# HGRN value tiles as one token-major group, and modulation products over 512 inputs per instruction, in a two-layer trunk kernel

## The chip, the cores and the metric

One core of a Trainium2 chip runs the whole kernel. The metric is the device time in microseconds (us) of one execution, the median of three runs. TensorE is called PE in the profile (its weight loads PEld), VectorE DVE, ScalarE ACT, GpSimd POOL, and SyncE, which here only issues transfers, SP.

## The reference

Two layers run over 640 tokens (128 of context, 512 latent) with a model width of 2048. Each layer modulates its input, makes one wide projection, feeds three branches from it, gates the branches and projects back:

```python
m = jax.nn.silu(cond) @ ada_w_l + ada_b_l            # "modulation": shift, scale, gate, 2048 each,
shift, scale, gate = jnp.split(m, 3, axis=-1)         # for two conditions (context, latent)
h = x * (1 + scale) + shift
z = h @ w_in_l                                        # 640 x 6656
aq, ak, av, ag, hq, hi, hff, hfb, hgate, ca, cb, cgate = jnp.split(z, SPLIT_POINTS, axis=-1)
v = hi.reshape(B, L, HG_HEADS, HG_DV)                 # HGRN values, 4 heads of 128
S_new = exp(g_last)[..., None] * S + einsum('bhsd,bhse->bhde', kc * exp(g_last - G), vc)
u = ca * jax.nn.sigmoid(cb)                           # conv branch: 31 taps, LayerNorm, silu
mix = concat([att * silu(ag), hg_out * silu(hgate), cv_out * silu(cgate)])
out = mix @ w_out_l
x_new = layer_norm(ALPHA * x + gate * out, ln_w_l, ln_b_l)
```

`hi` (512 columns) is the value of the HGRN branch; the scan needs it with tokens on the partitions.

## The kernel before

**Projection.** All products are in fp32, each operand split into a high and a low part, so that one product is three matmuls: input high by weight high (HH, wh), input low by weight high (HL, wh), input high by weight low. The 52 column tiles of 128 (`NTILES`, L32 ff.) are computed one after the other by `mm` (L1162 ff.): the weight tile is stationary, the 640 tokens stream as a matmul of 256 columns (L1173) and one of 384 (L1175), 16 k-blocks by 3, 48 pairs a tile. The result is feature-major (features on partitions) in one of two double banks `zt`. The tiles come in the order `hff, hfb, hi, hq` of the four heads, `hgate`, attention, `cb`/`ca`, `ag`, and at the end of the layer the four `cgate`.

**Weights.** Each tile's weights come in four chunks of 256 KB into the `RAW` slots (SP queue), and `ahead` splits the chunks of the next tile into the `WH` slots while this tile runs (ACT twice at L290/L291, and an accumulating DMA issued by POOL at L292).

**Everything else** is written as Python generators. `pump(3, rate)`, called after every half chunk, eight times a tile, lets up to three generators emit their next step, and also, `rate` times on the average, one step of the modulation job. The order in which the generators emit is the order in which each engine executes; nothing is reordered later. If a tile needs a free `zt` bank, `pump_until` (ahead of each tile) lets generators emit steps until one is free; where none can move, it takes a step of the modulation job instead.

**Slots.** Scratch comes from the pool `S` of 9 slots. `conv_ln` (L1030 ff.) holds the four conv sums and two more, `r` and `r2`, and at `summed()` takes two more at once, `S.getn`, before it can go on: a split (L287), PE sums over channels (L426, L427), 12 DVE products (L1068), squares on ACT (L1072), sums (L1046 to L1048), the same split and PE sums again, Ln (L1080), Exp (L1082), products (L1085), silu (L1091). `e_gate` takes one `S` slot before it evacuates its tile's `zt` bank (L1096), and holds it until the branch it gates is ready: for the `cgate` tiles this is the end of `conv_ln`.

**HGRN values.** `e_hi` evacuates a `hi` tile, and `to_tokens` turns it by five PE transposes (L474, L478), each copied out by ACT.

**Modulation.** The first layer's shift and scale are computed by PE at the start (`ada_pe`, L317 ff.; 16 steps of 256 features, on each of which `after0` builds part of the first layer's input). The other four parts are jobs of `ada_dve` (L336 ff.): two in layer 0 for its own gate and for layer 1's scale and shift among them, one in layer 1. A job has 64 raw weight blocks of 128x512 (256 KB, `adawD`), each multiplied with a row of the silu of a condition that is the same on all partitions (`crow`, 256 KB for 256 inputs of both conditions, L352), 4 products of 128x256 a block with a running sum (L362). A row occupies one `S` slot for 8 blocks, and the next one is loaded ahead, when half of the blocks are done.

**Start and boundary.** In the start three tiles run under `ada_pe` as its steps finish (`start_mm`). Between the layers, the last columns of the output projection (L1482) of each of the five token tiles are followed by `ln_next` (LayerNorm, modulation and transposes at L1384 of the next input), and next to it the first two tiles of the next layer run.

## Time and profile before

| what | value |
|---|---|
| median of three runs | 2241.13 us (2240.1 to 2241.21) |
| profiled execution, its own time | 2247.12 us |
| its span (first to last instruction) | 2245.3 us |
| PE busy / DVE / ACT / POOL | 97% / 65% / 51% / 27% |
| mean granted TensorE clock (share of 2.4 GHz) | 0.994 |

The profile is of one execution, so sums are made against its 2247.12 us and then set against the median. Busy shares come per engine; the page also gives them in forty slices of the span. The durations of matmuls overlap, since they are pipelined: what one costs is the distance from its start to the next one's start, which the timeline shows.

### The profile page before, as it was taken

The numbers are of one execution on the slowest core, as the hardware profiler recorded it, in microseconds if no ns is written. First come the engines' busy times: TensorE is split into PE (matmuls) and PEld (weight loads), VectorE is DVE, ScalarE is ACT, GpSimd is POOL, SyncE is SP. The second block draws the span as 40 slices with busy tenths as digits, with TensorE's granted clock in tenths as the row PEclk, the third lists the DMA queues.
The fourth block names the chain that finished last, engine by engine and source line by source line (L and its number), as shares of the span: only waits on it lengthen the run. The fifth ranks groups of instructions, "written<-read, shape, count | busy, mean of one in ns | idle before, by whom it ended". The sixth has DMA issues, their size and how long they took to land.

```text
span 2245.3 us, 42128 instructions
## 1 busy us (share of the span) xinstructions
PE 2177.4 (97%) x15854; PEld 2076.1 (92%) x15854; DVE 1457.9 (65%) x3799; ACT 1144.7 (51%) x2051; POOL 601.9 (27%) x690
## 2 busy tenths in 40 slices
PE   5899999999999999999989999999999999999997
PEld 2699999999999999988989999999999999998887
DVE  2478899557669999766673666543654779225457
ACT  1267877546565435511155787774555543462112
POOL 0033344332222343300032344433222123331003
PEclk9999999999999999999999999999999999999999
DMA  9978787897766888964426777778776576676333
GB/s 358 392 206 199 185 209 182 201 219 173 176 159 155 206 193 212 259 233 128 128 108 158 156 172 162 162 173 189 160 163 137 110 173 147 150 164 212 99 99 123
DMA packets 210557, 403.61 MB, mean 180 GB/s; under 512 B 24656, under 2 KB 30512, under 8 KB 209712
## 3 DMA queue, kind: packets, MB, share of 16 engines
q1 hardware_dynamic: 138992, 271.85, 38.4%
q0 software_dynamic: 61440, 116.96, 30.2%
q10 hardware_dynamic: 9920, 12.10, 1.7%
q8 instruction: 124, 2.03, 0.4%
q14 instruction: 81, 0.66, 0.1%
HBM read 383.46 MB, written 12.11 MB: 176 GB/s over the span
## 4 chain that ended last, share of the span: by engine, by line
PE 75%; DVE 9%; DMA 6%; issue 5%; ACT 3%; POOL 1%; ACTq 1%; SPq 0%; POOLq 0%; DVEq 0%
PE z L1175 29%; PE z L1173 19%; PE z L1431 9%; PE m L1431 8%; DVE junk L362 4%; DMA x<-adaw 2%; PE m L948 2%; PE m L1482 2%; PE m L862 1%; DMA s<-xT 1%; PE m L916 1%; DMA s<-s 1%; DMA wh<-win 1%; PE m L664 1%; ACT s L1391 1%
## 5 line engine op out<-in xcount | busy, mean ns | idle before, releaser
L1175 PE MATMUL z<-HH,wh 128*128 128x384 f32 x3296 | 1046.6, 339 | 0.0
L1173 PE MATMUL z<-HH,wh 128*128 128x256 f32 x3296 | 926.6, 283 | 1.9 <-DMA wh<-win 1.0
L292 POOL DMA_DIRECT2D wh<-win x388 | 345.2, 936 | 1095.3 <-ACT wh L291 1024.0
L1173 PEld LDWEIGHTS z<-HH,wh 128*128 128x128 f32 x3296 | 619.5, 189 | 5.8 <-DVE wh L287 1.6
L1175 PEld LDWEIGHTS z<-HH,wh 128*128 128x128 f32 x3296 | 620.6, 188 | 1.5
L1175 PE MATMUL z<-HL,wh 128*128 128x384 f32 x1648 | 558.2, 339 | 0.0
L362 DVE SCALAR_TENSOR_TENSOR junk<-raw,s 128x256 bf16<-128x256 f32 x1024 | 502.5, 491 | 53.2 <-DMA raw<-adawD 25.0
L1173 PE MATMUL z<-HL,wh 128*128 128x256 f32 x1648 | 461.6, 280 | 0.0
L1173 PEld LDWEIGHTS z<-HL,wh 128*128 128x128 f32 x1648 | 310.9, 189 | 0.0
L1175 PEld LDWEIGHTS z<-HL,wh 128*128 128x128 f32 x1648 | 310.4, 188 | 0.0
L291 ACT ACTIVATE wh<-wh 128x512 fp32r<-128x512 f32 x400 | 253.0, 633 | 78.5 <-PE z L1175 67.4
L290 ACT CAST wh<-raw 128x512 fp32r<-128x512 f32 x400 | 244.0, 610 | 72.0 <-issue 36.1
L286 ACT CAST wh<-raw 128x512 fp32r<-128x512 f32 x136 | 83.0, 621 | 305.0 <-PE m L1431 153.8
L1027 DVE SCALAR_TENSOR_TENSOR s<-s,sm,s 128x655 f32<-128x655 f32 x240 | 229.6, 957 | 6.3
L1431 PE MATMUL z<-wh,HH 128*128 128x512 f32 (+1 forms) x640 | 182.1, 368 | 0.0
L1431 PE MATMUL m<-wh,HH 128*128 128x512 f32 (+1 forms) x640 | 173.8, 357 | 0.0
L287 DVE TENSOR_TENSOR wh<-raw,wh 128x512 fp32r<-128x512 f32 x138 | 92.6, 687 | 119.5 <-ACT wh L286 119.5
L1431 PEld LDWEIGHTS z<-wh,HH 128*128 128x128 f32 x640 | 116.1, 189 | 20.1
L1431 PEld LDWEIGHTS m<-wh,HH 128*128 128x128 f32 x640 | 114.2, 189 | 17.6
L1431 PE MATMUL z<-wh,HL 128*128 128x512 f32 (+1 forms) x320 | 117.8, 368 | 0.0
L1431 PE MATMUL m<-wh,HL 128*128 128x512 f32 (+1 forms) x320 | 114.4, 358 | 0.0
L1096 ACT ACTIVATE s<-z 128x640 f32<-128x640 f32 x32 | 22.5, 703 | 152.5 <-PE z L1175 143.7
(561 smaller groups left out, 2718.6 us busy)
## 6 DMA issues: line engine op xcount, KB each, us to landing
raw<-win SPq DMA_DIRECT2D x416, 256.0 KB, 4.2
wh<-win POOLq DMA_DIRECT2D x388, 256.0 KB, 5.6
raw<-adawD SPq DMA_DIRECT2D x256, 256.0 KB, 4.2
x<-adaw SPq DMA_DIRECT2D x64, 512.0 KB, 8.3
raw<-wout SPq DMA_DIRECT2D x128, 256.0 KB, 2.7
s<-crow SPq DMA_DIRECT2D x32, 256.0 KB, 5.9
s<-xT ACTq DMA_DIRECT2D x16, 320.0 KB, 7.5
s<-s ACTq DMA_DIRECT2D x80, 64.0 KB, 3.9
```

The lines of the kernel that those rows point to most:

```text
L286: act.copy(hi, src)
L287: (lo_eng or dve).tensor_tensor(lo, src, hi.bitcast(F32), op=ALU.subtract)
L290: act.copy(hi, r)
L291: act.activation(lo, hi.bitcast(F32), AF.Copy, scale=-1.0)
L292: pool.dma_start(out=lo, in_=w.bitcast(F32R), accum_op=ALU.add)
L362: dve.scalar_tensor_tensor(junk, r[:, 256 * n:256 * n + 256], 1.0, rows[0][:, 256 * c:256 * c + 256], op0=ALU.mult, op1=ALU.mult, accum_ou ...
L948: pe.matmul(o, lhsT=v_, rhs=p_, start=(y == 0 and n_ == 0), stop=(y == len(bl) - 1 and n_ == 2))
L1027: dve.scalar_tensor_tensor(acc, u[:, t:t + AW], sm[:, cw + t:cw + t + 1], acc, op0=ALU.mult, op1=ALU.add)
L1173: pe.matmul(za, lhsT=w_, rhs=h_[:, 0:2, k, :], start=st_, stop=sp_)
L1175: pe.matmul(zb, lhsT=w_, rhs=h_[:, 2:5, k, :], start=st_, stop=sp_)
L1431: pe.matmul(bs[tt][:, 0:w], lhsT=h_[:, tt, k, :], rhs=w_[:, o:o + w], start=(k == 0 and n_ == 0), stop=(k == KT - 1 and n_ == 2))
L1482: pe.matmul(b[:, 0:w], lhsT=h_[:, tt, k, :], rhs=w_[:, o:o + w], start=(k == 0 and n_ == 0), stop=(k == KT - 1 and n_ == 2))
```

## The change

Two things change together.

The four `hi` tiles of a layer are no longer single tiles. They are computed as one group ahead of the 48 other tiles, with the input as the stationary operand and 512 weight columns streaming (`mm_hi`: 16 k-blocks, 5 token tiles, 3 matmuls of 512 columns, 240 a layer), so that the result has tokens on the partitions at once. `evac_hi` copies the five banks to where the output of the HGRN branch will be, and the separate value tile, `e_hi` and the transposes go. The order of tiles has the `hgate` tiles between the others, and the first tile goes to two single banks. At the start the group runs under `ada_pe` in place of the three tiles, with 16 weight chunks by the sixth of eight steps (12 before); at the boundary the group takes the place of the first two tiles, and its weight chunks 0 to 7 are split by POOL alone and by ACT with an accumulating DMA in turn.

In `ada_dve` a block is now multiplied by two products of 128x512 (one for each condition) in place of four of 128x256. A row is 512 inputs of one condition; two `S` slots hold both conditions' rows for 16 blocks, and the next two are taken and loaded where the former two are given back. Line numbers of the changed kernel are a few off: L362 is L371 there, L352 L365, L426/L427 L435/L436, L1068 L1062, L1173/L1175 L1167/L1169.

```diff
     def ada_dve(l, part):
         pi = ADAD.index((l, part))
-        rows, fly = deque(), deque()
-        tiles = [(kb, q) for kb in range(8) for q in range(8)]
-        nrow = nxt = 0
+        fly = deque()
+        tiles = [(kb, q) for kb in range(4) for q in range(KT)]
+        nxt = 0
         for kb, q in tiles:
...
-            if nrow <= kb or (nrow <= min(kb + 1, 7) and q == 4):
-                t = yield from S.get()
-                sync.dma_start(out=t[:, 0:512], in_=crow[nrow].rearrange("c k -> (c k)").partition_broadcast(P))
-                rows.append(t)
-                nrow += 1
-            yield
+            if q == 0:
+                rows = yield from S.getn(F32, F32)
+                for c in range(2):
+                    sync.dma_start(out=rows[c][:, 0:512], in_=crow[kb, c].partition_broadcast(P))
+                yield
             r = fly.popleft()
-            for n in range(2):
-                if n:
-                    yield
-                for c in range(2):
-                    o = 2 * (2 * q + n) + c
-                    dve.scalar_tensor_tensor(junk, r[:, 256 * n:256 * n + 256], 1.0, rows[0][:, 256 * c:256 * c + 256],
-                                             op0=ALU.mult, op1=ALU.mult, accum_out=aacc[:, kb, o:o + 1])
+            for c in range(2):
+                yield
+                o = 2 * q + c
+                dve.scalar_tensor_tensor(junk, r, 1.0, rows[c][:, 0:512], op0=ALU.mult, op1=ALU.mult,
+                                         accum_out=aacc[:, kb, o:o + 1])
             RAW.put(r)
-            if q == 7:
-                S.put(rows.popleft())
+            if q == KT - 1:
+                S.put(*rows)
...
+    def evac_hi(l, G):
+        h = outs[l][2]["h"].rearrange("p (j t) -> p j t", j=4)
+        for c in (1, 4, 0, 3, 2):
+            o, i = h[:, :, 128 * c:128 * c + 128], G[c].rearrange("p (j t) -> p j t", j=4)
+            if c > 2:
+                dve.tensor_copy(o, i)
+            else:
+                act.copy(o, i)
...
+    def mm_hi(l, G, k, tts):
+        hi, lo = wsp[l, k]
+        for tt in tts:
+            for n_, (h_, w_) in enumerate(((HH, hi), (HH, lo), (HL, hi))):
+                pe.matmul(G[tt], lhsT=h_[:, tt, k, :], rhs=w_, start=(k == 0 and n_ == 0),
+                          stop=(k == KT - 1 and n_ == 2))
...
     def start_mm(n):
-        for i in range(NS):
-            mm(0, i, zs[i], (2 * n, 2 * n + 1), (0, 1))
-            if n % 2:
-                WH.put(*wsp.pop((0, i, n // 2)))
+        for k in (2 * n, 2 * n + 1):
+            mm_hi(0, G, k, range(TT))
+            WH.put(*wsp.pop((0, k)))
...
-            rate = RATE[l][0 if i < 20 else 1 if i < 32 else 2 if i < 45 else 3]
+            rate = RATE[l][0 if i < 16 else 1 if i < 28 else 2 if i < 41 else 3]
...
-                    if not last and k < 8:
-                        w_split(l + 1, 0, k // 2, pool if k // 2 in LO0 else None, pool)
+                    if not last:
+                        if k % 4 == 1:
+                            w_split(l + 1, k // 2, pool, pool)
+                        else:
+                            w_split(l + 1, k // 2, "dma")
...
+                if tt == TT - 1:
+                    for k in range(2):
+                        mm_hi(l + 1, G, k, range(3))
...
-            mm(l + 1, 0, zt[0], range(KT), (0,))
-            g = ln_next(TT - 1)
-            for c in range(4):
-                w_split(l + 1, 1, c, pool if c in LO1 else None, pool)
-                next(g, None)
-            next(g, None)
+            for k in range(2, 8):
+                mm_hi(l + 1, G, k, range(3))
+            for _ in ln_next(TT - 1):
+                pass
```

The order in which the engines' instructions stand changes most at the end of layer 0's tiles. On DVE before, at the last of the conv branch's sums (L1048, `s_143` is `r`) and up to the first of the 12 products that follow it in `conv_ln`; raw is a weight block of the modulation job, `s_2825` and `s_3508` are its rows:

```order
L1047 TENSOR_TENSOR s_7282<-s_7715,s_1973 128x512
L1048 TENSOR_TENSOR s_143<-s_143,s_7282 128x640
L362 SCALAR_TENSOR_TENSOR junk,aacc<-raw_246,s_2825 128x256 x4
L362 SCALAR_TENSOR_TENSOR junk,aacc<-raw_166,s_3508 128x256 x4
L362 SCALAR_TENSOR_TENSOR junk,aacc<-raw_248,s_3508 128x256 x4
L287 TENSOR_TENSOR s_8607<-s_143,s_8606 128x640
L362 SCALAR_TENSOR_TENSOR junk,aacc<-raw_162,s_3508 128x256 x4
```

The same place in the changed kernel, `s_3457` being `r` and `s_141` and `s_7118` the two rows; first the beginning and then the end of the stretch between the sum (L1042) and the split (L300):

```order
L1041 TENSOR_TENSOR s_6110<-s_133,s_6710 128x512
L1042 TENSOR_TENSOR s_3457<-s_3457,s_6110 128x640
L371 SCALAR_TENSOR_TENSOR junk,aacc<-raw_246,s_141 128x512
L371 SCALAR_TENSOR_TENSOR junk,aacc<-raw_246,s_7118 128x512
L381 TENSOR_REDUCE s_137<-aacc 128x32
L382 SCALAR_TENSOR_TENSOR scl_81<-s_137,sm 128x32
```

```order
L371 SCALAR_TENSOR_TENSOR junk,aacc<-raw_166,s_7118 128x512
L371 SCALAR_TENSOR_TENSOR junk,aacc<-raw_246,s_141 128x512
L371 SCALAR_TENSOR_TENSOR junk,aacc<-raw_246,s_7118 128x512
L300 TENSOR_TENSOR s_8843<-s_3457,s_8842 128x640
L1062 SCALAR_TENSOR_TENSOR a00k<-m_103,s_5568 128x128
```

Twelve products stood between the sum and the split; now 130 do, and two instructions that end a job (L381, L382): a pair's rest of one job and all 128 of the next. On PE before, the first four of the eight channel sums of `conv_ln`, between two tiles' matmuls; the other four stand 132 tile matmuls later, and four more tiles follow these:

```order
L1173 MATMUL z_100<-HH,wh_234 128x256
L1175 MATMUL z_100<-HH,wh_234 128x384
L426 MATMUL m_102<-s_8606,ones 128x384
L427 MATMUL m_102<-s_8607,ones 128x384
L426 MATMUL m_103<-s_8606,ones 128x256
L427 MATMUL m_103<-s_8607,ones 128x256
L1173 MATMUL z_99<-HH,wh_235 128x256
L1175 MATMUL z_99<-HH,wh_235 128x384
```

And on PE in the changed kernel, between the last matmul of the third `cgate` tile (the 47th of the 48 tiles) and the first of the fourth:

```order
L1167 MATMUL z_100<-HH,wh_236 128x256
L1169 MATMUL z_100<-HH,wh_236 128x384
L435 MATMUL m_103<-s_8842,ones 128x384
L436 MATMUL m_103<-s_8843,ones 128x384
L435 MATMUL m_101<-s_8842,ones 128x256
L436 MATMUL m_101<-s_8843,ones 128x256
L435 MATMUL m_102<-s_8842,ones 128x384
L436 MATMUL m_102<-s_8843,ones 128x384
L435 MATMUL m_104<-s_8842,ones 128x256
L436 MATMUL m_104<-s_8843,ones 128x256
L1167 MATMUL z_99<-HH,wh_237 128x256
L1169 MATMUL z_99<-HH,wh_237 128x384
```

All eight channel sums now stand together, with no tile matmul between the first and the second half, and one tile behind them. On SP in the changed kernel, in the same stretch, at the change from one pair of rows to the next (L365; sixteen blocks on, the same pair of slots is loaded once more):

```order
L359 DMA raw_246<-adawD 128x512
L359 DMA raw_168<-adawD 128x512
L365 DMA s_141<-crow 128x512
L365 DMA s_7118<-crow 128x512
L359 DMA raw_162<-adawD 128x512
L359 DMA raw_316<-adawD 128x512
```

Before, a row was loaded between weight chunks, to a slot other than the one in use:

```order
L347 DMA raw_248<-adawD 128x512
L347 DMA raw_250<-adawD 128x512
L352 DMA s_3508<-crow 128x512
L1147 DMA raw_516<-wout 128x512
L347 DMA raw_518<-adawD 128x512
```

The two slots that the products read up to there are those that the next rows are loaded into, and no weight chunk stands between.

## Rows read from the trace of the kernel before

**Rows 1.** The page: busy us (share) and count by engine; PE in forty slices
```profile
PE 2177.4 (97%) x15854; PEld 2076.1 (92%) x15854; DVE 1457.9 (65%) x3799; ACT 1144.7 (51%) x2051; POOL 601.9 (27%) x690
PE   5899999999999999999989999999999999999997
```
**Rows 2.** Windows: from:to, length, busy us (count) by engine, clock, DMA share, GB/s
```profile
40.00:118.00 78.00, 63.40 (x619) 46.06 (x619) 32.84 (x80) 13.22 (x21) 0.00 (x0) 0.93 1.02 391
50.00:60.00 10.00, 7.47 (x46) 6.11 (x47) 3.79 (x9) 2.16 (x4) 0.00 (x0) 0.66 1.01 387
846.00:932.00 86.00, 85.40 (x583) 85.13 (x582) 75.30 (x268) 49.01 (x78) 30.93 (x33) 1.00 0.93 242
932.00:1126.00 194.00, 194.00 (x975) 165.97 (x974) 123.64 (x364) 44.01 (x72) 9.72 (x17) 1.00 0.55 169
1126.00:1185.00 59.00, 51.64 (x419) 49.23 (x419) 45.91 (x92) 36.00 (x92) 17.51 (x16) 1.00 0.35 127
```
**Rows 3.** Timeline of PE: start, duration us; a tile's matmul pairs, then output projection
```profile
400.09 0.28 PE L1173 MATMUL z<-HL,wh 128*128 128x256 f32 x1
400.38 0.28 PE L1173 MATMUL z<-HH,wh 128*128 128x256 f32 x1
...
999.70 0.39 PE L1431 MATMUL z<-wh,HH 128*128 128x512 f32 x1
999.93 0.39 PE L1431 MATMUL z<-wh,HL 128*128 128x512 f32 x1
```
**Rows 4.** Transposes of value tiles by line: count | busy us, mean ns | idle before
```profile
L474 PE MATMUL m<-ident,s 128*128 128x128 f32 x32 | 4.8, 272 | 0.0
```
**Rows 5.** DVE by line, and the timeline of modulation products after the conv sums
```profile
L362 DVE SCALAR_TENSOR_TENSOR junk<-raw,s 128x256 bf16<-128x256 f32 x1024 | 502.5, 491 | 53.2 <-DMA raw<-adawD 25.0 <-DMA s<-crow 3.4
L1337 DVE SCALAR_TENSOR_TENSOR y1y<-y1y,z 128x512 f32<-128x512 f32 x8 | 5.5, 687 | 0.3
L1337 DVE SCALAR_TENSOR_TENSOR y1y<-y1y,m 128x256 f32<-128x256 f32 x8 | 3.4, 421 | 0.3
...
853.92 0.42 DVE L362 SCALAR_TENSOR_TENSOR junk<-raw,s 128x256 bf16<-128x256 f32 x1
854.38 0.43 DVE L362 SCALAR_TENSOR_TENSOR junk<-raw,s 128x256 bf16<-128x256 f32 x1
```
**Rows 6.** DMA issues of the page: KB each, median us to landing
```profile
raw<-adawD SPq DMA_DIRECT2D x256, 256.0 KB, 4.2
s<-crow SPq DMA_DIRECT2D x32, 256.0 KB, 5.9
```
**Rows 7.** Timelines of DVE, then ACT: the conv branch's LayerNorm in layer 0
```profile
857.55 0.82 DVE L287 TENSOR_TENSOR s<-s,s 128x640 fp32r<-128x640 f32 x1
862.23 0.29 DVE L1068 SCALAR_TENSOR_TENSOR a00k<-m,s 128x128 f32<-128x128 f32 x1 [0.25 <-PE m L427]
868.78 0.83 DVE L1048 TENSOR_TENSOR s<-s,s 128x640 f32<-128x640 f32 x1
...
882.18 0.95 ACT L1080 ACTIVATE s<-m,eps 128x384 f32<-128x384 f32 x2 [2.45 <-PE m L427]
890.12 0.91 ACT L1091 ACTIVATE a01v<-a01v,sm 128x640 f32<-128x640 f32 x1
893.28 0.69 ACT L1096 ACTIVATE s<-z 128x640 f32<-128x640 f32 x1
```
**Rows 8.** PE's waits in 40 to 118 us: us in total, times, longest
```profile
PE m L317 <- DMA x<-adaw: 8.1, 9, 2.0
PE m L327 <- DVE s L323: 6.6, 12, 0.6
```
**Rows 9.** PE in 118 to 1126 us, the first HGRN matmul, by line
```profile
L540 PE MATMUL m<-s,s 128*32 128x32 f32 x640 | 9.0, 200 | 7.7 <-DVE s L534 4.5 <-DVE s L607 3.2
```
**Rows 10.** PE's waits in 1126 to 1185 us, the boundary of the layers
```profile
PE m L1384 <- ACT s L1391: 4.5, 6, 1.8
PE m L1384 <- ACT y0y L1375: 1.9, 1, 1.9
```

More of the change, by code (lines that the diff above doesn't have):

```diff
@@ L168, in trunk @@
     M = Free(mb)
-    crow = drp.tile([8, 2, 256], F32, name="crow")
+    crow = drp.tile([4, 2, 512], F32, name="crow")
     gsc = drp.tile([2, 2, D], F32, name="gsc")
@@ L186, in open_layer @@
     def open_layer(l):
-        outs[l] = region(f"o{l}", "left", [(f"h{j}", T) for j in range(4)])
+        outs[l] = region(f"o{l}", "left", [("h", 4 * T)])
         for j in range(4):
-            mix[l, 8 + j] = outs[l][2][f"h{j}"]
+            mix[l, 8 + j] = outs[l][2]["h"][:, T * j:T * j + T]
         for st in range(2):
@@ L310, in ada_pe @@
                 if nxt == W0:
[L311 to L312 removed]
+                    w_load(0, *range(4))
             if kq == 0:
@@ L452, in e_hf @@
         kd = Kt[:, T * d:T * d + T]
-        act.activation(kd, zsb(z), AF.Sigmoid, scale=-1.0)
+        for x, v_ in zparts(z):
+            act.activation(kd[:, x], v_, AF.Sigmoid, scale=-1.0)
         zput(z)
@@ L505, in hg_main @@
     def hg_main(l, j):
-        yield from wait(("hf", l, j, 0), ("hf", l, j, 1), ("hi", l, j), ("hq", l, j))
+        yield from wait(("hf", l, j, 0), ("hf", l, j, 1), ("hq", l, j))
         lk = yield from lock["hg"].get()
         st = hgset[l, j]
-        Kt, GG, q, v = hv(l, st)
+        Kt, GG, q, v = hv(l, st, j)
         ae = aE[j % 2]
@@ L1111, in evac, with w_src, w_load, w_split @@
             return e_gate(l, j + {"ag": 0, "hgate": 8, "cgate": 12}[name], z)
-        return {"hi": e_hi, "hq": e_hq, "ak": e_ak, "av": e_av, "aq": e_aq, "cb": e_cb, "ca": e_ca}[name](l, j, z)
+        return {"hq": e_hq, "ak": e_ak, "av": e_av, "aq": e_aq, "cb": e_cb, "ca": e_ca}[name](l, j, z)
     wraw = {}
-    def w_load1(l, i, c):
-        pump_until(lambda: RAW.f)
-        r = RAW.take()
-        sync.dma_start(out=r, in_=A["win"][l, i, c])
-        wraw[l, i, c] = r
-    def w_load(l, i):
-        for c in range(4):
-            w_load1(l, i, c)
+    def w_src(l, q):
+        return A["whi"][l, q] if q < NG else A["win"][l, q - NG]
+    def w_load(l, *qs):
+        for q in qs:
+            pump_until(lambda: RAW.f)
+            r = RAW.take()
+            sync.dma_start(out=r, in_=w_src(l, q))
+            wraw[l, q] = r
     wsp = {}
-    def w_split(l, i, c, lo_eng=None, hi_eng=None):
+    def w_split(l, q, lo_eng=None, hi_eng=None):
         pump_until(lambda: len(WH.f) >= 2)
         hi, lo = WH.take(), WH.take()
-        r = wraw.pop((l, i, c))
+        r = wraw.pop((l, q))
         if lo_eng == "dma":
-            split_add(hi, lo, r, A["win"][l, i, c])
+            split_add(hi, lo, r, w_src(l, q))
         else:
             split(hi, lo, r, lo_eng, hi_eng)
-        wsp[l, i, c] = (hi, lo)
+        wsp[l, q] = (hi, lo)
         RAW.put(r)
@@ L1233, in enqueue, with ahead @@
                 active.append(conv_ln(l))
-        first = NS if l == 0 else 2
-        wnext = 4 * (first + 2)
-        def ahead(i, c):
+        wnext = NG + 8
+        def ahead(q):
             nonlocal wnext
-            m = 4 * (i + 1) + c
-            if i + 1 < NN:
-                w_split(l, i + 1, c, "dma")
+            m = q + 4
+            if m < NQ:
+                w_split(l, m, "dma")
             else:
-                o_split(l, c)
+                o_split(l, m - NQ)
             while wnext <= m + (WLH if 0 in hold else WLA):
-                if wnext < 4 * NN:
-                    w_load1(l, wnext // 4, wnext % 4)
+                if wnext < NQ:
+                    w_load(l, wnext)
                 else:
-                    o_load(l, wnext - 4 * NN)
+                    o_load(l, wnext - NQ)
                 wnext += 1
-        for i in range(first):
-            enqueue(i, zs[i] if l == 0 else zt[i])
-        for i in range(first, NN):
-            pump_until(lambda: ZP.f)
-            z = ZP.f.popleft()
+        M.f = deque(mb[3:])
+        evac_hi(l, G)
+        for i in range(NN):
+            if i == 0:
+                z = Z(mb[0], mb[1])
+            else:
+                pump_until(lambda: ZP.f)
+                z = ZP.f.popleft()
             if i == HOLD0:
                 hold.add(0)
-            rate = RATE[l][0 if i < 20 else 1 if i < 32 else 2 if i < 45 else 3]
+            rate = RATE[l][0 if i < 16 else 1 if i < 28 else 2 if i < 41 else 3]
             for c in range(4):
@@ L1471, in trunk @@
             affine_consts()
-            w_load(l + 1, 0)
-            w_load(l + 1, 1)
-            obank = [mb[2], zh[1], zh[3], zh[1], zh[3]]
-            banks = deque(mb[3:] + mb[:3])
+            w_load(l + 1, *range(8))
+            G = [zl[0], zl[1], mb[2], zf[0], zf[1]]
+            obank = [mb[2], zl[0], zf[0], zl[0], zf[0]]
+            banks = deque(mb[3:] + mb[:2])
         for tt in range(TT):
```

140 lines of the change are left out of this document (63 added, 77 removed).

## The prediction

> **What bounds the kernel now.** I read the page first: PE is busy 97% of the span and the slices show it at 9 nearly everywhere, with an unfilled start and end [rows 1]. So a change helps where it takes columns from PE or fills PE's few gaps, and hurts where it makes PE wait; DVE, at 65%, has time to spare on the average. Next the windows, since an average hides stages [rows 2]: at the end of layer 0's tiles (846 to 932 us) PE is busy 85.4 of 86 us, while DVE is at 75.3, so DVE's work there is covered, but only because tiles run beside it. In the output projection behind them (932 to 1126) PE is busy all of the time. The start is another regime: from 40 to 118 us the DMA share is 1.02 at 391 GB/s and PE is busy 63.4 of 78 us; its waits are for modulation weights (8.1 us) and for a DVE step (6.6 us) [rows 8]. The boundary of the layers (1126 to 1185) leaves PE 7.4 us idle, 6.4 of them before the transposes of the next input [rows 2, 10]. Small waits in the first HGRN matmul come to 7.7 us in layer 0 [rows 9].
>
> The prices: a pair of a tile takes 0.29 us from start to start, so a tile of 48 pairs takes 14.0 us; a matmul of 512 columns takes 0.23 [rows 3].
>
> **The change part by part.** The sum is made against the profiled 2247.1 us.
>
> *A, the start.* The three tiles (42 us of PE) become the group of four tiles: 240 x 0.227 = 54.5 us, 1.6 less than four tiles at 14.03. So 12.4 us of PE work more is done under the start, and is gone behind it. Against this: 4 more weight chunks by the sixth step, 1 MB at 391 GB/s = 2.7 us on a stage that DMA bounds [rows 2]; what is left when the last modulation step is done, two steps of `start_mm`, is 2 x 30 x 0.227 = 13.6 us where it was 2 x 18 x 0.292 = 10.5 (a step had two k-blocks of three tiles, 18 pairs), +3.1; and not all of 12.4 us fits in PE's 14.7 us of waits, since those for DVE are of 0.6 us each and stay: +1. -12.4 + 2.7 + 3.1 + 1 = **-5.6**. Bounds: -9 if the tail is covered, +1 if nothing fits in.
>
> *B, transposes.* 40 go from PE. Their busy time is 4.8 us for 32 [rows 4], 0.15 each, 6 us for 40; half of a 256-column distance [rows 3] would be 0.06 each, 2.4. I take **-4**. ACT loses the copies, which were not waited for.
>
> *C, the boundary.* The group saves 1.6 again. Behind the last token tile's columns stand 72 group matmuls (16 us) ahead of the last `ln_next`, where one half of a tile, 48 x 0.12 = 5.6 us, stood before; this can hide up to 6.4 us of waits for ACT [rows 10]. But the chunks split with ACT and an accumulating DMA add two ACT instructions and a landing of about that of a weight block, 4 to 6 us [rows 6], each, to an engine that PE waits for there. Between -6 (waits gone) and +8 (one of those chunks late, twice) I take **+1**.
>
> *D, HGRN waits.* Values are ready at once, and the branch's DVE chain (L534, L607) is untouched; the waits of 7.7 us [rows 9] can shrink, or grow as the branch starts one tile earlier after the start. **-2**, between -6 and +3.
>
> *E, modulation products.* One product of 128x256 takes 0.46 us from start to start [rows 5]. A 512-wide DVE product of the same kind takes 687 ns where the 256-wide takes 421 [rows 5], 0.27 more: so 0.73 each, and the job of 128 takes 93 us of DVE where 256 took 118. All 512 save about 100 us of DVE, which are on no path while PE is busy beside them: nothing, by the windows [rows 2].
>
> What costs is where they stand. The job now holds two `S` slots throughout, with six in `conv_ln` and one in a `cgate` tile: nine of nine. `conv_ln` needs two more for its sums and cannot have them until the job ends. Before, two were free (six, one row, at most one row ahead), so it went on at once, which the order shows: 12 products between its sum and its split. Now 130 stand there. The `cgate` tiles cannot free their banks: the third needs a slot too, and the fourth tile needs a bank. Then `pump_until` has nothing else to move, and takes the rest of the job at once, in front of all of `conv_ln`. The sum stands in the code's order some 4.6 tiles before this point, at 9 to 10 products a tile; about 48 of the 130 go under the tiles, **82 are forced**, with no tile matmul beside them, as PE's order confirms: all eight channel sums between the third and the fourth `cgate` tile. In sequence, PE waits for:
> - 82 products x 0.73 = 59.9 us;
> - two changes of rows: the slots are the ones in use, so the load can start only behind the last product that reads them, and the next product waits for it: 2 x 5.9 [rows 6], 12 us;
> - the rest of `conv_ln` up to the gate that frees a bank, from its parts [rows 7]: split and sums, 0.7 + 0.8 + 0.6 = 2.1; from the first product to the end of the squares' sum 862.23 to 869.61, less two modulation products in it, 6.5; the second split and sums 2.1; from Ln to the end of the last silu 882.18 to 891.03, less two weight copies on ACT of 1.2, 7.6; the gate's silu 0.7. Together 19, with hand-overs 20 us;
> - less what DVE has done of this when PE ends the third `cgate` tile. The weight blocks share their slots with the tiles' chunks, and most of the forced products depend on one that is freed as that tile begins; so the lead is at most one tile, 14 us; I take 10.
>
> 59.9 + 12 + 20 - 10 = **+82**. Bounds: 68 (0.69 each, row loads as fast as blocks at 4.2, a rest of 17, a full lead), and 107 (0.78 each, 10 for two rows on one queue, 23, no lead). The last tile, 14 us, and the output projection follow as before: nothing later is waiting that could take the stall up, since PE is full there. Layer 1 has one job and more slots free at this point; there the eight sums stand apart, as before.
>
> *F, the clock.* Between 50 and 60 us, with PE waits of up to 2 us, PE's granted clock was 0.66 on the average [rows 2, 8], a mixture of 2.4 and 1.2 GHz: 7.5 us busy of which a third is the slower clock's, 2.5 us. PE will be idle far longer in E, once: **+2**, between 0 and 4.
>
> A rule that speaks against the change. DVE is not saturated here: 65% of the span, and PE's gaps are few [rows 1]. The Trainium skill, "Perfetto Trace Analysis", "Optimizing Scalar/DVE Operations", says that larger operations help an engine that is saturated, and that where one that is not causes bubbles on others, smaller instructions may let work end sooner. By this rule the merging gains nothing here. The same section gives about 60 ns of overhead for a DVE instruction in SBUF; by that figure two 256-wide products of 0.46 merge into one of about 0.87 (an estimate), the burst takes 71 us, and the time would be 11 us above mine. The rows give a direct pair of widths, and I go by them.
>
> Sum: -5.6 - 4 + 1 - 2 + 82 + 2 = +73.4; 2247.1 + 73.4 = 2320.5. The profiled execution was 6.0 us above the median, so **2314.5 us**.
>
> **The rivals.**
> - *No stall: the forced products run ahead.* Engines go by their own queues; if DVE reaches the burst while PE is still four or five tiles back, the tiles cover it. For it: DVE is idle a third of the time [rows 1], and products, rows and rest together, 92 us, would fit beside seven tiles. Against it: slots tie the weight blocks to tiles that PE has finished, and DVE was 88% busy there [rows 2]. It decides from a lead of 92 us, and the lead is at most 14. The time would be 2241.1 - 10.6 = 2230.5, faster than before. Chance 0.04.
> - *A shorter burst.* If a 512-wide product with a running sum costs what a 256-wide does (0.46; no row shows one of this width), the burst is 38 us, and the time 2293. For it: nothing but the missing row. The rows for other operations speak against it. With the lead of a full tile also 2289. Chance 0.1.
> - *A longer burst, by transfers.* Each block of 256 KB must land in 1.46 us, 180 GB/s, with three in flight at 4.2 us each [rows 6]: 1.4 us, just enough. If a block takes 2.0 us, as when it queues behind rows, the burst becomes 82 us: 2337. DMA share is below 1 there [rows 2], against it. Chance 0.14.
> - *No change.* The gains of A to D (-10.6) meet a stall of the same size, if only a job's rest of a dozen products were forced: 2241. The order of instructions, which is fixed, is against it. Chance 0.02.
>
> **How the numbers follow.** The forecast has 0.7. The range takes in the shorter and the longer burst, and E's bounds in so far as not all ends meet at once: 2289 to 2342. A measurement here tells apart about 0.2%, 4.5 us. Faster: the first rival, 0.04; same: 0.02; slower: 0.94.
>
> **What would show it.** In the profile after: one PE gap of 75 to 100 us before the last `cgate` tile of layer 0, near 900 us, with DVE in unbroken 512-wide products of 0.7 us, SP's two row loads in it, and the chain of waits through them. No such gap in layer 1. The first tile's matmuls start with some 6 us less of work left behind the start. If the gap is there but the products are shorter or the rows cost nothing, the size in E was wrong; if the gap is missing, its mechanism.

## The result, and the profile after

The changed kernel takes 2334.78 us (median of four runs, 2333.76 to 2335.91), against 2240.88 us before: 1.042 times the time, with a 95% interval of 1.0402 to 1.0438, 94 us slower. The forecast was 2314.5 us, in a range of 2289 to 2342.

The page of the changed kernel, busy us and shares, and PE and its clock in forty slices:

```profile
PE 2176.6 (93%) x15526; PEld 2053.3 (88%) x15526; DVE 1379.5 (59%) x2785; ACT 1129.0 (48%) x2028; POOL 595.1 (25%) x680
PE   6899899999999996099998998999999999999997
PEclk9999999999999998599999999999999999999999
```

PE has about as much busy time as before [rows 1] in a longer span, and one of the forty slices, 58 us long, in which it does nothing. The windows around that slice (from:to, length, busy us and count by engine, clock, DMA share, GB/s) and what PE waited for there:

```profile
846.00:912.00 66.00, 66.00 (x452) 66.00 (x451) 37.69 (x98) 22.26 (x38) 20.86 (x24) 1.00 0.98 255
912.00:976.00 64.00, 0.43 (x3) 0.17 (x1) 54.40 (x155) 0.58 (x1) 0.00 (x0) 0.53 0.63 179
976.00:996.00 20.00, 3.77 (x9) 2.38 (x9) 11.66 (x24) 13.18 (x18) 3.82 (x3) 0.50 0.07 23
996.00:1012.00 16.00, 16.00 (x94) 16.00 (x95) 6.69 (x9) 9.30 (x17) 4.88 (x5) 0.84 0.59 132
```
```profile
PE m L435 <- ACT s L299: 71.5, 2, 63.8
PE z L1167 <- ACT s L1090: 7.9, 1, 7.9
```

The two waits for L299 are those for the two splits of `conv_ln`, the third is the one for the gate's silu that frees a bank. They are 79.4 us. In the first of them DVE alone has work. Its timeline there (start, duration, line, what ended the idle time before), with the two changes of rows and the end of the burst:

```profile
912.19 0.69 DVE L371 SCALAR_TENSOR_TENSOR junk<-raw,s 128x512 bf16<-128x512 f32 x1 [1.08 <-DMA raw<-adawD]
912.92 0.69 DVE L371 SCALAR_TENSOR_TENSOR junk<-raw,s 128x512 bf16<-128x512 f32 x1
...
921.73 0.69 DVE L371 SCALAR_TENSOR_TENSOR junk<-raw,s 128x512 bf16<-128x512 f32 x1
925.20 0.69 DVE L371 SCALAR_TENSOR_TENSOR junk<-raw,s 128x512 bf16<-128x512 f32 x1 [2.77 <-DMA s<-crow]
926.35 0.69 DVE L371 SCALAR_TENSOR_TENSOR junk<-raw,s 128x512 bf16<-128x512 f32 x1 [0.45 <-DMA s<-crow]
...
948.36 0.69 DVE L371 SCALAR_TENSOR_TENSOR junk<-raw,s 128x512 bf16<-128x512 f32 x1
952.49 0.69 DVE L371 SCALAR_TENSOR_TENSOR junk<-raw,s 128x512 bf16<-128x512 f32 x1 [3.43 <-DMA s<-crow]
953.41 0.69 DVE L371 SCALAR_TENSOR_TENSOR junk<-raw,s 128x512 bf16<-128x512 f32 x1 [0.23 <-DMA s<-crow]
...
975.42 0.69 DVE L371 SCALAR_TENSOR_TENSOR junk<-raw,s 128x512 bf16<-128x512 f32 x1
976.23 0.82 DVE L300 TENSOR_TENSOR s<-s,s 128x640 fp32r<-128x640 f32 x1
```

To see where else time went, both timelines of PE are laid side by side by work done: the start of the same matmul tile, counted from the end of the first four tiles (or of the group).

| point | before, us | after, us | after minus before | step |
|---|---|---|---|---|
| four tiles / the group done, layer 0 | 142.53 | 129.57 | -13.0 | -13.0 |
| 24 tiles on (HGRN and first attention) | 551.44 | 545.60 | -5.8 | +7.1 |
| 46 tiles on | 905.99 | 898.19 | -7.8 | -2.0 |
| last tile of layer 0 | 920.07 | 995.84 | +75.8 | +83.6 |
| first matmul of layer 0's output projection | 935.54 | 1013.80 | +78.3 | +2.5 |
| four tiles / the group done, layer 1 | 1230.45 | 1308.54 | +78.1 | -0.2 |
| 24 tiles on | 1629.39 | 1718.92 | +89.5 | +11.4 |
| PE's end | 2233.05 | 2321.88 | +88.8 | -0.7 |

The table compares one profiled execution of each kernel, and that of before lay 6.0 us above its median; so its steps add up to 88.8 us where the medians differ by 93.9, and a single step can be off by some us.

So there are two losses: the stall, as forecast, and one of 18.5 us in the HGRN stretches of both layers, which was not. In the second one PE has one long wait in each layer, 7.9 us in layer 0 and 8.0 in layer 1. The wait in layer 0, and the windows around it:

```profile
PE m L567 <- DVE s L528: 7.9, 1, 7.9
```
```profile
200.00:240.00 40.00, 36.70 (x336) 36.02 (x334) 26.48 (x56) 31.21 (x52) 16.02 (x18) 1.00 0.74 171
240.00:280.00 40.00, 34.71 (x382) 33.88 (x383) 32.90 (x52) 31.62 (x53) 16.57 (x18) 0.87 0.71 170
```

In the 40 us from 240 on, the end of the wait and what follows it, the granted clock is 0.87 on the average. DVE's timeline there shows what stands ahead of the product that PE wants (L528, the second head's second level):

```profile
232.94 0.82 DVE L528 SCALAR_TENSOR_TENSOR s<-s,h01q 128x640 f32<-128x640 f32 x1
...
242.79 0.89 DVE L715 SCALAR_TENSOR_TENSOR o0h<-o0h,sm,s 128x640 f32<-128x640 f32 x1 [8.42 <-ACT s L713]
243.59 0.82 DVE L527 TENSOR_TENSOR s<-s,h01kt 128x640 f32<-128x640 f32 x1
244.33 0.81 DVE L528 SCALAR_TENSOR_TENSOR s<-s,h01q 128x640 f32<-128x640 f32 x1
```

L715 is the last product of the first head's norm: it waits 8.4 us for ACT, and the second head's products stand behind it.

### The profile page after: what moved, and what is told of

The parts are those of the page before. It is cut to its first block, busy times and chain, and to the rows that moved or that the text cites. A ratio compares the mean times of both kernels' runs of the same rounds, so it can differ in the third digit from the quotient of the medians.

```text
span 2334.1 us, 40462 instructions
## 1 busy us (share of the span) xinstructions
PE 2176.6 (93%) x15526; PEld 2053.3 (88%) x15526; DVE 1379.5 (59%) x2785; ACT 1129.0 (48%) x2028; POOL 595.1 (25%) x680
## 4 chain that ended last, share of the span: by engine, by line
PE 73%; issue 7%; ACT 6%; DVE 5%; DMA 5%; POOL 3%; ACTq 0%; SPq 0%; POOLq 0%; DVEq 0%
PE z L1169 25%; PE z L1167 17%; PE z L1427 8%; PE m L1427 8%; PE z L1175 3%; DVE junk L371 3%; DMA x<-adaw 2%; PE m L942 2%; PE m L856 1%; PE m L1478 1%; DMA s<-crow 1%; PE m L910 1%; POOL s L515 1%; ACT wh L303 1%; PE m L1175 1%
## 5 line engine op out<-in xcount | busy, mean ns | idle before, releaser
L1169 PE MATMUL z<-HH,wh 128*128 128x384 f32 x3008 | 959.6, 339 | 0.0
L1167 PE MATMUL z<-HH,wh 128*128 128x256 f32 x3008 | 850.6, 283 | 9.7 <-ACT s L1090 7.9
L305 POOL DMA_DIRECT2D wh<-win x380 | 335.4, 928 | 1154.7 <-ACT wh L304 1078.0
L1167 PEld LDWEIGHTS z<-HH,wh 128*128 128x128 f32 x3008 | 567.5, 189 | 14.1 <-ACT s L1090 8.2
L1169 PEld LDWEIGHTS z<-HH,wh 128*128 128x128 f32 x3008 | 567.5, 189 | 1.5
L1169 PE MATMUL z<-HL,wh 128*128 128x384 f32 x1504 | 509.8, 339 | 0.0
L371 DVE SCALAR_TENSOR_TENSOR junk<-raw,s 128x512 bf16<-128x512 f32 x512 | 400.8, 783 | 67.2 <-DMA s<-crow 32.6
L1167 PE MATMUL z<-HL,wh 128*128 128x256 f32 x1504 | 421.1, 280 | 0.0
L1167 PEld LDWEIGHTS z<-HL,wh 128*128 128x128 f32 x1504 | 283.7, 189 | 0.0
L1169 PEld LDWEIGHTS z<-HL,wh 128*128 128x128 f32 x1504 | 283.5, 188 | 0.0
L299 ACT CAST wh<-raw 128x512 fp32r<-128x512 f32 x144 | 87.9, 621 | 299.1 <-PE m L1427 159.4
L300 DVE TENSOR_TENSOR wh<-raw,wh 128x512 fp32r<-128x512 f32 x144 | 96.2, 687 | 180.5 <-ACT wh L299 175.0
```

Of the source, the lines that this page charges most:

```text
L299: act.copy(hi, src)
L300: (lo_eng or dve).tensor_tensor(lo, src, hi.bitcast(F32), op=ALU.subtract)
L305: pool.dma_start(out=lo, in_=w.bitcast(F32R), accum_op=ALU.add)
L371: dve.scalar_tensor_tensor(junk, r, 1.0, rows[c][:, 0:512], op0=ALU.mult, op1=ALU.mult, accum_out=aacc[:, kb, o:o + 1])
L1167: pe.matmul(za, lhsT=w_, rhs=h_[:, 0:2, k, :], start=st_, stop=sp_)
L1169: pe.matmul(zb, lhsT=w_, rhs=h_[:, 2:5, k, :], start=st_, stop=sp_)
```

## The experiments

Theory: wide products with two row slots held without a break keep `conv_ln` from its slots, and cause the stall. Rival: the new order of tiles does. The second question is what the HGRN loss comes from.

**1 and 2. The two parts apart.** The first kernel has the value group and its order of tiles, with `ada_dve`, `crow` and `adawD` as before. The second has the new `ada_dve` alone:

```diff
 # first: the changed kernel, with
-            for c in range(2):
-                yield
-                dve.scalar_tensor_tensor(junk, r, 1.0, rows[c][:, 0:512], ...)
+            for n in range(2):
+                for c in range(2):
+                    dve.scalar_tensor_tensor(junk, r[:, 256 * n:256 * n + 256], 1.0, rows[0][:, 256 * c:256 * c + 256], ...)
 # second: the kernel before, with the opposite edit
```

> The group of value tiles with the order of tiles of the changed kernel; modulation products as before (256 wide, one row slot). Theory (the wide products' second slot makes the stall): the stall of 80 us before the last cgate tile is gone; what is left are the start (-13.0 against before), the HGRN stretches (+7.1 and +11.4), the late tiles (-2.7) and the boundary (+2.3), all read from the changed kernel's trace: 2241 + 5 = 2246 us, 2240 to 2252. Rival (the new order of tiles alone leaves conv_ln without its slots): the stall stays, 2325 to 2340 us.

> The modulation products over 512 inputs alone, with value tiles and the order of tiles as before. Theory: the stall comes with the wide products alone. Here about 96 products stand in front of conv_ln's first split at the last cgate tile: 96 x 0.733 = 70.4, rows 2 x 3.5 = 7, the rest of conv_ln 20, less a lead of 4, and 2 for the clock: +95, 2336 us (2325 to 2345). Rival (the stall needs the new order of tiles): 2241 us, within 5.

The group alone took 2271.49 us (ratio 1.0135, 1.012 to 1.0151), the wide products alone 2315.88 (1.034, 1.0322 to 1.0357). PE's waits at the end of layer 0's tiles with the wide products alone:

```profile
PE m L423 <- ACT s L286: 63.0, 2, 55.3
PE z L1170 <- ACT s L1093: 7.9, 1, 7.9
```

and with the group alone:

```profile
PE z L1170 <- DMA wh<-win: 1.2, 1, 1.2
PE m L439 <- DVE s L300: 1.2, 1, 1.2
```

So the stall belongs to the wide products; the rival falls. The wide products cost 20 us less than expected: the stall was 71 us of waits, and not the 93 that I had worked out for 96 products (66 of them started while PE stood still), and their trace was 10 us ahead of the kernel before when it reached the stall. The group costs 25 us more than expected: in its trace the stretch of 24 tiles in layer 0 is 19.7 us longer than before, and the one in layer 1 13.1, together 14 more than in the changed kernel. Another 6 come from the reckoning: it added to the median of before differences against its profiled execution, which lay 6.0 us higher.

**3. Giving the slots away.**

```diff
             if q == KT - 1:
                 S.put(*rows)
+                yield
```

> The changed kernel with one step of pause between giving back a pair of row slots and taking the next pair, so that another generator can take them between. Theory (slots held without a break keep conv_ln waiting): conv_ln goes on at once, the 80 us stall and its slow restart are gone, -83.6; as the job pauses meanwhile, some 28 of its products are left to the end of the output projection, where they cost between 0 and 20: 2251 to 2271 us. Rival (it is the amount of products in that place, wherever the slots are): the wait turns up elsewhere, over 2300 us.

2269.92 us (1.0134, 1.0119 to 1.0149), in the expected range. From 900 to 1000 us no wait of PE is left in the trace. The time not won back stands at the boundary, as expected:

```profile
PE m L1381 <- DVE y0y L1370: 17.5, 1, 17.5
```

There the job's last 26 products are one unbroken piece of 19 us on DVE, ahead of the norm that PE waits for. So it was not the amount of products, and not DVE's load: one pause of one step ends the stall.

**4. The norm product out of the way.**

```diff
-        lock["hg"].put(lk)
         for _ in range(RY):
             yield
...
         S.put(sq)
+        lock["hg"].put(lk)
         flags.add(("mix", l, 8 + j))
```

> The changed kernel, but the next HGRN head may start only after the last product of the former head's norm (the lock is given back behind it), so that this product no longer stands between the next head's first and second pair of level products on DVE. Theory (PE waits 8.1 us in each layer for the second pair, which waits in DVE's queue behind the norm product, which waits for ACT's Exp): both waits go, with the time lost at the lower clock behind them, -18 to -24: 2311 to 2317 us. Rival (the head comes too early for its own exponentials, which ACT and POOL deliver late): the wait stays or moves, 2330 to 2340 us.

2337.9 us (1.0438, 1.0422 to 1.0453): nothing won. The wait became three, of the same sum:

```profile
PE m L534 <- DVE s L528: 4.8, 1, 4.8
PE m L567 <- DVE s L528: 1.8, 1, 1.8
PE m L562 <- DVE s L528: 1.6, 1, 1.6
```

My theory on the one instruction fell, as the rival said. In PE's order the second head's first matmul now stands 1.0 tiles behind the first head's last one, 0.4 more than in the changed kernel, where before it was 1.6.

**5. More distance between the heads**, in the first run's kernel:

```diff
-NTILES = ([(n, j) for j in (0, 1) for n in ("hff", "hfb", "hq")] + [("hgate", 0)]
-          + [(n, 2) for n in ("hff", "hfb", "hq")] + [("hgate", 1)]
-          + [(n, 3) for n in ("hff", "hfb", "hq")] + [("hgate", 2), ("hgate", 3)]
+NTILES = ([(n, 0) for n in ("hff", "hfb", "hq")]
+          + [t for j in (1, 2, 3) for t in (("hff", j), ("hfb", j), ("hgate", j - 1), ("hq", j))] + [("hgate", 3)]
```

> The kernel of the first run (value group, modulation products as before, 2271 us), with one thing changed: the order of the HGRN tiles, so that the heads' last tiles are four tiles apart (hff, hfb, hgate of the head before, hq) and each head starts about 0.9 tiles after the former head ends, as in the kernel before, and not at once. Theory (the heads follow each other too closely: a head's chain on POOL, ACT and DVE starts while these still work off the head before, and PE, which follows 5 half chunks behind, waits and then runs at the lower clock): the loss around the second head, 10 to 16 us a layer, goes: 2240 to 2252 us, less if the later end of the last head costs something. Rival (the loss belongs to the group itself, for the branch has three tiles beside it where it had four): no change, 2266 to 2275 us.

2269.13 us (1.0127, 1.011 to 1.0144): no change in the total, which is the rival's figure, but not for the rival's reason. The stretches of 24 tiles were, against before, +25.5 us in layer 0 and +0.4 in layer 1 (+19.7 and +13.1 without the distance). In layer 1 the theory held and the loss was gone. What was won there was lost in two other places. The boundary of the layers took 10.5 us longer than before (-0.2 in the first run), with one wait for the next layer's norm that the first run did not have:

```profile
PE m L1382 <- DVE y0y L1371: 7.9, 1, 7.9
```

And in layer 0 three heads waited, 16.2 us together; there DVE's and POOL's timelines show another cause at 258.95 us:

```profile
258.95 5.88 DVE L530 SCALAR_TENSOR_TENSOR s<-s,h01q 128x640 f32<-128x640 f32 x1
```
```profile
258.74 1.57 POOL L517 TENSOR_TENSOR s<-h01gg 128x640 f32<-128x640 f32 x1
260.11 1.48 POOL L520 TENSOR_TENSOR s<-h01gg 128x640 f32<-128x640 f32 x1
261.41 1.39 POOL L517 TENSOR_TENSOR s<-h01gg 128x640 f32<-128x640 f32 x1
262.62 1.51 POOL L520 TENSOR_TENSOR s<-h01gg 128x640 f32<-128x640 f32 x1
```

A product of 0.8 us lasts 5.9: it ends 0.7 us behind the last of four subtractions on POOL. The same happens to one product of each of the two heads that follow (5.88 and 5.89 us), and PE waits for all three.

**6. The rate of the modulation steps**, in the third run's kernel:

```diff
-RATE = ((1.0, 0.85, 0.5, 1.2), (0.5, 0.5, 0.0, 0.8))
+RATE = ((1.0, 0.85, 0.5, 2.0), (0.5, 0.5, 0.0, 0.8))
```

> The kernel of the third run (the change with one step of pause between pairs of rows, 2270 us), with a higher rate of modulation steps in the last stretch of layer 0's tiles (2.0 and not 1.2 a call). Theory: the 28 products that were left to the end of the output projection, and stood as one piece of 20 us on DVE in front of the next layer's norm (PE waited 17.7 us), are done earlier beside tiles: -15 to -19, 2251 to 2256 us. Rival (DVE has no room for them beside the last tiles, and they delay conv_ln there): 2262 us or more.

2268.01 us (1.0125, 1.011 to 1.014), as the rival said, though not where it said: the wait of 17.5 us went, `conv_ln` was not delayed, and the products now stood at the start of the output projection, ahead of the splits of its input:

```profile
PE m L1428 <- DVE HL L300: 7.0, 1, 7.0
PE z L1168 <- DMA wh<-win: 2.8, 1, 2.8
PE m L1428 <- ACT HH L299: 2.4, 1, 2.4
```

**7. All of it**: the sixth run's kernel, the fifth's order of tiles, and at the boundary one chunk split in another way:

```diff
-                            w_split(l + 1, k // 2, "dma")
+                            w_split(l + 1, k // 2, *(() if k == 3 else ("dma",)))
```

> Value group, wide products with the pause and the higher rate, the heads four tiles apart, and at the boundary the second of the group's weight chunks split by ACT and DVE and not by ACT and an accumulating DMA (PE waited 4.5 us for that). Theory: the parts add: 2253 (the run beside it) - 20 to -28 for the heads of both layers - 4 for the boundary: 2221 to 2233 us, below the kernel before. Rival (the heads' loss is the group's own): 2246 to 2252 us.

2259.21 us (1.0088, 1.0073 to 1.0103), above both ranges. They counted with 2253 for the sixth run, which took 2268; against that it is 9 us less, where the theory had 20 to 32 and the rival 1 to 7. No head's product is waited for longer than 1.4 us now, and the boundary's wait fell from 4.5 to 0.8. What took the heads' place came at their end: the last head holds its slots until the 18th tile, and the first key tile, which takes three slots before it frees its bank, waits; PE waits for that (L753) 4.6 us in layer 0 and 4.8 in layer 1.

**8 and 9. The fourth head earlier, and fewer products beside the heads.**

```diff
 # both
-RWO = 4 / 3
+RWO = 2.0
-RATE = ((1.0, 0.85, 0.5, 2.0), (0.5, 0.5, 0.0, 0.8))
+RATE = ((0.6, 1.2, 0.7, 1.2), (0.0, 0.8, 0.5, 0.8))
 # the eighth alone: ... hff 3, hfb 3, hq 3, hgate 2, hgate 3 in place of hff 3, hfb 3, hgate 2, hq 3, hgate 3
```

> The seventh run's kernel (2259 us) with two changes: the first three HGRN heads four tiles apart, the fourth three tiles behind the third, so that the first key tile no longer waits for the slots that the last head holds; and the modulation steps less in the HGRN tiles (0.6 and 0.0 a call in the two layers), more among the attention tiles, and 2.0 and not 4/3 a call in the output projection. Theory: the waits for the key tile's slots (4.9 + 1.5 us and the lower clock behind them, in each layer) and those at the start of the output projection (7.2 + 2.5) go: -22 to -26; the fourth head, again directly behind the third, costs 8 to 11 a layer, as the second did: 2249 to 2258 us. Rival (with few modulation products in DVE's queue beside the heads, a close head costs little): 2232 to 2242 us.

> The seventh run's kernel (2259 us) with its order of tiles, and only the rates of the modulation steps as in the run beside it. Theory: the waits at the start of the output projection go (-8 to -10), those for the key tile's slots stay: 2248 to 2252 us. Rival (the modulation products lengthen the heads' chains on DVE): another 4 to 8 us less in the HGRN stretches, 2241 to 2247 us.

The eighth took 2242.5 us (1.0011, 1.0001 to 1.0021), the ninth 2244.78 (1.0023, 1.0013 to 1.0033), each at its rival's figures or half a us above them. In both, PE has no wait left at the start of the output projection, and the rates alone (the ninth run against the seventh) are worth 14 us. The 24 tiles of layer 1 cost +10.8 in the seventh run, +5.3 in the eighth and +7.9 in the ninth.

**10. The wide products alone, with the pause.** The second run's kernel with

```diff
                 S.put(*rows)
+                yield
-RWO = 4 / 3
+RWO = 2.0
-RATE = ((1.0, 0.85, 0.5, 1.2), (0.5, 0.5, 0.0, 0.8))
+RATE = ((1.0, 0.85, 0.45, 1.2), (0.5, 0.5, 0.0, 0.8))
```

> The wide modulation products alone, as in the second run (value tiles and the order of tiles as before), with the pause between pairs of rows, and rates (0.45 and not 0.5 a call among the conv tiles, 2.0 and not 4/3 in the output projection) by which conv_ln gets its slots at once. Theory: without the stall the wide products are worth what the second run's trace showed ahead of it, about 10 us against the profile of before, of which some 8 in layer 0's start and HGRN tiles (fewer DVE instructions in the heads' chains); since that profile lay 6 us above the runs without a profile, 2229 to 2237 us. Rival (DVE is off the path, its time is worth nothing, as in the prediction): 2240 us, within 3.

2235.22 us (0.9971, 0.9961 to 0.9982), in the theory's range: 6.4 us less than the kernel before, and the best of all. Its window of the end of layer 0's tiles, and its row for the first HGRN matmul:

```profile
846.00:932.00 86.00, 85.89 (x562) 83.86 (x561) 57.02 (x127) 52.67 (x85) 27.20 (x29) 1.00 0.90 228
```
```profile
L538 PE MATMUL m<-s,s 128*32 128x32 f32 x640 | 9.0, 199 | 1.7 <-DVE s L605 0.9 <-DVE s L532 0.7
```

PE is as busy there as before [rows 2] with DVE at 57 and not at 75 us, and the waits of the heads in layer 0 fell from 7.7 us [rows 9] to 1.7. The rates were changed too; in the HGRN tiles, where the waits went, they are as before. By the points of the table, the stretch of 24 tiles in layer 0 is 9.9 us shorter than before, the start 2.5, and all else differs by less than 2; up to 6 us of this can come from the profiled execution of before, which lay that much above its median.

**11. The gate job's transpose later**, in the eighth run's kernel:

```diff
         if part == 2:
-            yield
-            yield
-            yield
+            for _ in range(10):
+                yield
```

> The eighth run's kernel (2242 us), in which the gate job's PE transpose stands ten and not three steps behind the DVE reduction that it needs. Theory: PE's wait of 5.3 us for it in layer 0, and the lower clock behind, go: 2235 to 2238 us, just below the kernel before. Rival (PE waits there for something else of the attention on DVE, and will wait in the next place): 2240 to 2243 us.

2246.97 us (1.0024, 1.0015 to 1.0033), above both ranges. The wait of 5.1 us went, and two smaller ones came (2.2 and 1.7 us, for DVE in the attention); from the last tile of layer 0 to the end of the next group it took 5 us longer, and which of the steps that slid by seven places did that was not tried.

**12. The changed kernel's own order of tiles, with the eighth run's rates.**

> The eighth run's kernel (2242 us) with the changed kernel's own order of tiles, in which the second HGRN head follows the first at once and the others with a gap: the rates of the modulation steps are those of the eighth run. Theory (what costs is the closeness of a head to the one before): PE's wait of 8 us for the second head's products is back in both layers, with the lower clock behind it, but the waits of the close fourth head go, 3 us a layer: 2253 to 2262 us. Rival (what costs is the modulation products in DVE's queue beside the heads, which the rates have taken away, wholly in layer 1): 2238 to 2246 us, with the wait gone in layer 1.

2251.38 us (1.0046, 1.0029 to 1.0063), two below the theory's figures and well above the rival's. In layer 1, where these rates leave no modulation product beside the heads, the wait is back whole:

```profile
PE m L568 <- DVE s L529: 8.1, 1, 8.1
```
```profile
1325.79 0.82 DVE L529 SCALAR_TENSOR_TENSOR s<-s,h11q 128x640 f32<-128x640 f32 x1
1335.67 0.88 DVE L716 SCALAR_TENSOR_TENSOR o1h<-o1h,sm,s 128x640 f32<-128x640 f32 x1 [9.05 <-ACT s L714]
1336.47 0.82 DVE L528 TENSOR_TENSOR s<-s,h11kt 128x640 f32<-128x640 f32 x1
1337.20 0.82 DVE L529 SCALAR_TENSOR_TENSOR s<-s,h11q 128x640 f32<-128x640 f32 x1
```

So the second head's wait of 8 us comes from its closeness to the first, and not from the products between. In time it makes less than 8 us a layer: the stretches of 24 tiles are +10.5 and +9.7 us against before here, and +7.6 and +7.9 in the ninth run, whose heads are four tiles apart at the same rates, since another wait stands there in its place (4.8 us for the key tile's slots in each layer).

## Why the prediction was right

The mechanism was right in each part: slots that are nine of nine, a bank that cannot be freed, the rest of a job forced in front of `conv_ln`, and PE idle before the last tile. It is shown by runs 1, 2 and 3: without the wide products, and with them but with one pause, the stall is gone, and with them alone it is there. Layer 1 has no such gap, as forecast. Point by point, as the sum had them:

- **E, the burst: forecast +82, measured +83.6** (the last tile's step: 79.8 us in which PE is idle, and 3.8 of channel sums). Product: 912.92 less 912.19 is 0.73 us, as worked out from the two widths of another product [rows 5]. Rows: DVE's two waits at each change are 2.77 + 0.45 and 3.43 + 0.23 us, 7 together and not 12; the four row loads there landed 3.4 to 4.2 us after their issue, faster than the median of 5.9 before [rows 6]. The rest of `conv_ln`: from the end of the last product at 976.1 to the first matmul of the last tile at 995.84, 19.7 for 20. The lead: of the 82 products 78 start behind PE's last matmul of the third `cgate` tile, so DVE was four products ahead, 3 us and not 10; it had just waited 1.08 us for a weight block. Two errors of 5 and 7 us cancelled, which is luck.
- **F, the clock: +2, measured +2.5.** The last tile, from its first matmul to that of the output projection, took 17.96 us where it was 15.47 before, with a granted clock of 0.84 in the 16 us behind the stall. The working has a slip: an average of 0.66 between the two levels is two thirds of the time at the lower one, not a third; the cost, 2.5 us, comes out the same.
- **A, the start: -5.6, measured -13.0.** The mis-sized part is what I added for DMA and for PE's room. PE's waits for the modulation weights fell from 8.1 us [rows 8] to 2.7, and its clock rose from 0.93 [rows 2] to 1.00, so the additional matmuls filled gaps in which the clock had fallen, and the 1 MB more of weights did not show. Not all of the 13.0 is the group's: it is -11.3 in run 1, which has the group alone, -8.7 in run 5, which starts in the same way, and in runs 2 and 10, whose start has the three tiles of before, the same point also came 2.9 and 2.5 us earlier than in the profile of before. PE's waits and the window:

```profile
PE m L339 <- DVE s L335: 6.6, 12, 0.5
PE m L329 <- DMA x<-adaw: 2.7, 4, 0.8
```
```profile
40.00:118.00 78.00, 68.69 (x585) 45.44 (x584) 34.58 (x84) 14.88 (x24) 0.00 (x0) 1.00 0.99 390
```

- **C, the boundary: +1, measured -0.2** from the first matmul of the output projection on. As bounded: the waits for ACT shrank from 6.4 us [rows 10] to 3.5, and one chunk split by an accumulating DMA came late:

```profile
PE z L1175 <- DMA wh<-whi: 4.5, 1, 4.5
PE m L1380 <- ACT s L1387: 3.5, 5, 0.8
```

- **B and D, transposes and HGRN waits: -6 together, measured +18.5.** This step failed. I had the branch's chain as untouched, and its instructions are; what changed is their place. The group takes a tile out of each head's stretch, and only between the first two heads does no `hgate` tile fill the gap: in PE's order 1.6 tiles lay between the first head's last matmul and the second head's first one, and now 0.6. Runs 5 (layer 1), 7 and 12 show that the wait of 8 us goes with distance and comes back with closeness; run 4 shows that the norm's product ahead of it is not what makes it. That closeness makes up all of the 18.5 is not shown. The loss is gone in one place only, layer 1 of run 5 (+0.4). Elsewhere, with all heads four tiles apart, other waits stand in its place: both stretches together cost 15.3 us in run 7 and 15.5 in run 9, with 4.6 to 4.8 us in each layer for the last head's slots, and layer 0 of run 5 cost 25.5, with 16.2 us for products that POOL held up. What each of these takes of the rest is not settled.
- **E's other half, merged products at no worth: wrong by the tenth run**, which is 6 us faster than the kernel before. That the DVE time was saved on a path, the heads' chains in layer 0, is likely and not shown apart from the rest: the waits went there (7.7 to 1.7 us), and the same stretch with the group was +19.7 with the narrow products (run 1) and +7.1 with the wide ones. The part of the Trainium skill that was weighed, "Perfetto Trace Analysis", "Optimizing Scalar/DVE Operations", says that larger operations can help where the engine is saturated. DVE is not (65%), and they helped all the same; the measurement decides. By the section's figure of 60 ns an instruction a product would take 0.87 us (an estimate); it took 0.73.
- **From the profiled execution to the median: -6.0, measured -1.1** (2335.91 against 2334.78). The profile before happened to lie above all its other runs, 6.0 us above their median; those of the other kernels lay from 4 us below to 5 above their medians. So 5 us of the difference between the medians stand in no step of the table, and which stretch of that one execution took longer is not known.

The misses: -7.4 (A), +24.5 (B, D), -2.7 (the last tiles), +1.6 (E), +0.5 (F), -1.2 (C) and +4.9 make +20.2, the difference between 2314.5 and 2334.8. The largest is the HGRN loss. That the time still fell into the range is in part luck: the range reached up to 2342 for a longer burst, which did not come, and a loss that was not forecast took up that room.

## What to carry to other kernels

Where the order of instructions is fixed when the code is written, count the scratch slots at each place where something takes several of them at once: a background job that holds its slots without a break can turn into the foreground, and a single pause between giving back and taking again ended a stall of 80 us, which was worth 65 us of the kernel's time. Where a stage is taken out between two uses of the same engines, look at what the distance did for them, not only at what the stage cost. An engine with a third of its time free may still be worth relieving: look for short chains through it that end at the engine that bounds.

## What the runs showed of the hardware

A DVE product of two operands in SBUF can be not slowed by POOL's subtractions but held: 5.88 us for 0.81 of work, to the end of four of them in a row (run 5, in three heads). The Trainium skill, "SBUF — State Buffer", "Who interferes with whom", has it that a DVE instruction with two SBUF inputs contends with a GpSimd instruction that reads SBUF, and that the ports they share are an exclusive lock. The trace agrees, and shows that the hold can last beyond a single instruction of the other side. Which product is caught is a matter of phase: in the kernel before it was one that nobody waits for, a modulation product (L362, whose mean of 491 ns [rows 5] is above the 420 of the undisturbed ones), while the same four subtractions ran for the second head:

```profile
223.70 6.16 DVE L362 SCALAR_TENSOR_TENSOR junk<-raw,s 128x256 bf16<-128x256 f32 x1
```

In run 5 it was one that PE needs.
